# Splitting the first two output tiles of the second MLP product, adding weight pairs by DMA, and moving statistics and small tiles in a one-core decoder block

## Chip, cores and metric

The kernel runs on one core of one Trainium2 chip. The metric is the device time of one execution in microseconds (us). The kernel before was run three times: 751.61, 751.81 and 756.94 us, median 751.81 us.

## What is computed

One decoder block on 512 tokens of width 1024, in float32. A causal pooling mixer and a causal differential attention are merged by sigmoid gates, a cross-attention on a memory of 256 rows follows, then the MLP and a final norm. What bears on the change is the end:

```python
    x = x + memory_cross_attention(hc, mem_n, w_cq[l], w_ckv[l], w_co[l])
    hm = rms_norm(x, g_mlp[l])
    x = x + jnp.square(jax.nn.relu(hm @ w_up[l])) @ w_down[l]
return rms_norm(x, g_final)
```

w_up is 1024 x 4096 and w_down 4096 x 1024.

## The kernel before

Activations stand transposed: 128 features on the partitions, 512 tokens along a row. Every float32 operand is split into a high part (float32r, a cast on ScalarE, `S.copy` in `split`, line 110) and a low part (the difference, on VectorE, line 111), and every product takes three matmuls: high by high, high by low, low by high (`mm3`, lines 104 to 106).

**The MLP** is done in NG = 4 groups of 1024 hidden features. The first product of a group is two sets, n = 2g and 2g+1. A set is a Winograd form of the 2 x 2 block product: seven block products instead of eight. Its left factors are blocks of the weights and sums of them, in the order `ORDER` (for n = 0 `FIRST_ORDER`): A11, s1 = A21 + A22, s2 = s1 + A11, s3 = A21 + A11, A12, A22, s4 = s2 + A12. The names fit the code and not the signs, which lie in the right factors. The four sums are made by VectorE in `combined` (lines 169, 170, 174, 178) from raw blocks that SyncE's DMA queue loads into the tiles `mraw` (five buffers); s1 and s2 stand in `wraw` (three buffers), which also takes the raw weights of all other products. `prep` then splits each block into a pair of tiles, `whi`/`wlo` (three buffers each) or `mhl` (four, so two pairs). `weights(i)` is called when block i comes up on TensorE: it asks for loads up to seven blocks ahead and for splits up to four blocks ahead; five split blocks fit, so a split waits until the block five places before it has been used.

The right factors (B11, T1, T2, T3, B21, B22, T4) are made by `right_factors(m, t)` for each of the eight feature tiles m as the cross-attention's output product (`projection("co", ...)`) finishes it: for m < 4, B11 and T1; for m >= 4, T2 and T3 (lines 772 and 773 and a split), B21 and B22 (a split), T4 (line 781 and a split). `accumulate` adds the tile's squares to `ss2`. After the last tile `split_sq` splits ss2, and `stats2` sums it over the partitions by two matmuls with a matrix of ones (lines 230, 231) and makes 1/rms, `r2`. TensorE's order is the order of the code. `stats2` is put into it by a count of steps, `after(STAT2, ...)`: a block product is four steps, so with STAT2 = 8 it comes after the first two block products (A11 and s1). The order on the other engines is laid out by the compiler's planner, and each of them runs its queue strictly in that order.

`up_set` adds up the seven products (line 871), multiplies by r2 and takes the square of the positive part (`squared_relu`, lines 846 and 847), and splits the result into `act`: entries 0 to 3 from the even set, 4 to 7 from the odd one. Entries 6 and 7 are complete after A22, entries 4 and 5 only after s4, the set's last block.

The second product of a group ("dn") has eight output tiles m. Each is 24 matmuls of 512 columns over act 0 to 7 in order, into one of two PSUM banks `acc`; then `residual` (line 567) adds it to the running x. In the last group tile 7 is done in two halves, with the final norm behind it.

Of the kernel before, what the change touches and what calls it, by code (L numbers as in the profile page):

```python
# [14 lines left out]
ALU = mybir.AluOpType  # L15
# [17 lines left out]
MEMIN, EARLY, LATE = 16, [4, 5, 6, 0, 1], [2, 7, 3]  # L33
WARM = 8
ON_POOL = (1, 3, 5, 7), (1, 3, 5)
STAT1, STAT2, STATM = 16, 8, 20
PARTS = "A11", "A12", "A21", "A22"
ORDER = "A11", "s2", "s1", "s3", "A12", "A22", "s4"
FIRST_ORDER = "A11", "s1", "s2", "A12", "s3", "A22", "s4"
# [10 lines left out]
def block_kernel(ctx: ExitStack, tc: tile.TileContext, x0g, xT, memT, wv, wm, wst, wckv, wpool, vecs, csts, outT):  # L50
# [24 lines left out]
    def sb(tag, shape, bufs, dt=F32):  # L75
        p = apool if tag in EARLY_TAGS else late["pool"] if tag in LATE_TAGS else pool
        return p.tile(shape, dt, tag=tag, name=nm(tag), bufs=bufs)
# [13 lines left out]
    def acc():  # L91
        return ps("acc", 2)
# [16 lines left out]
    def split(hi, lo, src, eng=V):  # L109
        S.copy(hi, src)  # L110
        eng.tensor_tensor(lo, src, f(hi), op=ALU.subtract)  # L111

    vx = sb("vx", [P, NG_COL + T + 19], 1)[:, :NG_COL + T]
    vec = vx[:, :NG_COL]
    cst = sb("cst", [P, NCST], 1)
    nc.sync.dma_start(vx, x0g)
# [6 lines left out]
    warm = ps("acc", 2)  # L123
    for j in range(WARM):
        nc.tensor.matmul(warm, idle[:, :P], idle, start=j == 0, stop=j == WARM - 1)
    eps = sb("eps", [P, 32], 1)[:, :1]
    V.memset(eps, EPS)
    one_f = sb("onef", [P, P], 1)
    V.memset(one_f, 1.0)
# [14 lines left out]
    def fetch(key, src, tag, bufs):  # L144
        if key not in raw:
            raw[key] = sb(tag, [P, D], bufs)
            nc.sync.dma_start(raw[key], src)
        return raw[key]

    def load(i):  # L150
        if i >= len(blocks):
            return
        if isinstance(blocks[i], tuple):
            n, name = blocks[i]
            for part in {"A11": ("A11",), "s1": ("A21", "A22"), "s2": ("A21", "A22"), "A12": ("A12",)}.get(name, ()):
                fetch((n, part), wst[4 * n + PARTS.index(part)], "mraw", 5)
        elif i == 0 and i not in raw:
            r = raw[i] = sb("wraw", [P, D], 3)
            nc.sync.dma_start(r[:, :T], blocks[i][:, :T])
            load_x(1)  # L160
            nc.sync.dma_start(r[:, T:], blocks[i][:, T:])
        else:
            fetch(i, blocks[i], "wraw", 3)

    def combined(n, name):

        if (n, "s1") not in raw and name in ("s1", "s2"):
            s1, s2 = sb("wraw", [P, D], 3), sb("wraw", [P, D], 3)
            V.tensor_tensor(s1, raw[n, "A21"], raw[n, "A22"], op=ALU.add)
            V.tensor_tensor(s2, s1, raw[n, "A11"], op=ALU.add)  # L170
            raw[n, "s1"], raw[n, "s2"] = s1, s2
        elif name == "s3":
            r = raw[n, "A21"]
            V.tensor_tensor(r, r, raw[n, "A11"], op=ALU.add)
            return r
        elif name == "s4":
            r = raw[n, "s2"]
            V.tensor_tensor(r, r, raw[n, "A12"], op=ALU.add)
            return r
        return raw[n, name]  # L180
# [52 lines left out]
    def rstd_full(sp, scratch, w=T):  # L233
        o = ps("tr", 2)[:, :w]
        bcast_sum(o, *sp)
        r = sb("rstd" if w == T else "mrstd", [P, w], 1)
        rsqrt(r, o, 1.0 / D, scratch, tmp()[:, :w])
        return r

# [11 lines left out]
    def accumulate(ss, k, src, w=T):  # L251
        if k == 0:
            S.activation(ss, src, AF.Square)
        else:
            sq = tmp()[:, :w]
            S.activation(sq, src, AF.Square)
            V.tensor_tensor(ss, ss, sq, op=ALU.add)
# [28 lines left out]
    def tile_mm(o, w, rhs, ks=range(KC), first=True, last=True):  # L286
        ks = list(ks)
        for n, k in enumerate(ks):
            c = slice(k * P, (k + 1) * P)
            mm3(o, w[0][:, c], w[1][:, c], rhs[k][0], rhs[k][1],  # L290
                first and n == 0, last and n == len(ks) - 1)
            tick()
# [60 lines left out]
    def lambdas():  # L353
        lvec = tmp()[:, :NVEC]
        nc.gpsimd.dma_start(lvec, vecs)
        lam = sb("lam", [P, 4], 1)
        lsum = sb("lsum", [P, 4], 1)
        for j in range(2):
            b = 128 * j
            V.tensor_tensor(lvec[:, b:b + 64], lvec[:, b:b + 64], lvec[:, b + 64:b + 128], op=ALU.mult)  # L360
            V.tensor_reduce(lsum[:, j:j + 1], lvec[:, b:b + 64], axis=AX.X, op=ALU.add)
            S.activation(lam[:, j:j + 1], lsum[:, j:j + 1], AF.Exp)
        V.tensor_tensor(lam[:, 2:3], lam[:, 0:1], lam[:, 1:2], op=ALU.subtract)
        V.tensor_scalar(lam[:, 3:4], lam[:, 2:3], LAM_INIT, None, op0=ALU.add)
        gsub = sb("gsub", [P, 16], 1)[:, :1]
        V.tensor_scalar(gsub, vec[:, GSUB:GSUB + 1], 1.0 - LAM_INIT, None, op0=ALU.mult)
        st["lam"], st["gsub"] = lam[:, 3:4], gsub

# [196 lines left out]
    def residual(m, o, g=None, ss=None, nxt=None, tag=None):  # L565
        t = res[m]
        V.tensor_tensor(t, o, t, op=ALU.add)  # L567
        if ss is None:
            return
        pr = pair(tag, 8)  # L570
        scaled(pr[:, 0, :], pr[:, 1, :], t, vec[:, g + m:g + m + 1])
        accumulate(ss, m, t)
        nxt[m] = (pr[:, 0, :], pr[:, 1, :])
# [168 lines left out]

    ss2 = sb("ss", [P, T], 1)
    right = {n: {} for n in ("B11", "T1", "B21", "B22", "T2", "T3", "T4")}
    xs, half = {}, {}
    A, B = slice(0, M), slice(M, T)

    def parts(name, k, hi, lo, c):
        right[name][k] = (hi[:, c], lo[:, c])

    def right_factors(m, t):

        k = m % 4
        g = vec[:, G_MLP + m:G_MLP + m + 1]
        x = tmp()
        pr = pair("mix", 8)
        if m < 4:
            if k % 2 == 0:
                half["B12"] = tmp()
            b12 = half["B12"][:, k % 2 * M:k % 2 * M + M]  # L760
            S.activation(x[:, A], t[:, A], AF.Copy, scale=g)
            S.activation(b12, t[:, B], AF.Copy, scale=g)
            V.tensor_tensor(x[:, B], x[:, A], b12, op=ALU.subtract)
            xs[k] = (x[:, B], b12)
            split(pr[:, 0, :], pr[:, 1, :], x)
            parts("B11", k, pr[:, 0, :], pr[:, 1, :], A)
            parts("T1", k, pr[:, 0, :], pr[:, 1, :], B)
            return
        S.activation(x, t, AF.Copy, scale=g)
        t1, b12 = xs[k]  # L770
        y = tmp()
        V.scalar_tensor_tensor(y[:, A], x[:, B], -1.0, t1, op0=ALU.mult, op1=ALU.subtract)
        V.tensor_tensor(y[:, B], x[:, B], b12, op=ALU.subtract)
        p2 = pair("s", 6)
        split(p2[:, 0, :], p2[:, 1, :], y)
        parts("T2", k, p2[:, 0, :], p2[:, 1, :], A)
        parts("T3", k, p2[:, 0, :], p2[:, 1, :], B)
        split(pr[:, 0, :], pr[:, 1, :], x)
        parts("B21", k, pr[:, 0, :], pr[:, 1, :], A)
        parts("B22", k, pr[:, 0, :], pr[:, 1, :], B)  # L780
        V.scalar_tensor_tensor(y[:, A], y[:, A], -1.0, x[:, A], op0=ALU.mult, op1=ALU.subtract)
        if k % 2 == 0:
            half["T4"] = pair("s", 6)
        c = slice(k % 2 * M, k % 2 * M + M)
        split(half["T4"][:, 0, c], half["T4"][:, 1, c], y[:, A])
        parts("T4", k, half["T4"][:, 0, :], half["T4"][:, 1, :], c)

    def done_co(m, o):
        residual(m, o)
        right_factors(m, res[m])  # L790
        accumulate(ss2, m, res[m])

    def renew():

# [65 lines left out]
    def up_set(n, act, j0):  # L860
# [12 lines left out]
        for name in FIRST_ORDER if n == 0 else ORDER:  # L873
# [23 lines left out]
            elif name == "s4":  # L897
                u["C12"] = u["U4"]
                plus("C12", o, "U4")
                squared_relu(*x, u["C12"], B)  # L900

    for g in range(NG):
        act = {}
        for n in (2 * g, 2 * g + 1):
            up_set(n, act, 4 * (n % 2))
        for m in range(KC):
            last = g == NG - 1
            w = W("dn", g, m)
            if last and m % 2 == 0:
                y3[m // 2] = sb("mix", [P, 2, T], 8)  # L910
            if last and m == KC - 1:
                st["sp3"] = split_sq(ss3, T)
                for hf, o in enumerate((ps("sc", 3), ps("sc", 3))):
                    c = slice(hf * M, (hf + 1) * M)
                    tile_mm(o[:, c], w, {k: (a[:, c], b[:, c]) for k, (a, b) in act.items()})
                    last_rows(m, o, c)
                flush()
                continue
            o = acc()
            tile_mm(o, w, act)  # L920
            residual(m, o)
            if last:
                accumulate(ss3, m, res[m])
                S.activation(y3[m // 2][:, m % 2, :], res[m], AF.Copy,
                             scale=vec[:, G_FINAL + m:G_FINAL + m + 1])


def _mtiles(w):
# [70 lines left out]
```

## Time and profile before

| | |
|---|---|
| median of 3 runs | 751.81 us |
| profiled execution, its time | 758.01 us |
| profiled execution, its span | 756.2 us |
| mean granted TensorE clock | 0.978 |
| TensorE busy | 722.5 us (96%) |
| VectorE busy | 530.7 us (70%) |
| ScalarE busy | 393.9 us (52%) |
| GpSimd busy | 58.8 us (8%) |
| moved by DMA | 78.51 MB |

In the profile PE is TensorE's matmul, PEld its weight load, DVE VectorE, ACT ScalarE, POOL GpSimd and SP SyncE; SPq and POOLq are the issuing queues. L111 is line 111 of the kernel. A wait's row gives who waited (engine, tile, line), for whom, the total, the number of times and the longest. A window's row gives each engine's busy time in that stretch with the number of its instructions, the granted clock and the DMA engines' share. Matmuls overlap in their pipeline, so a matmul's duration (0.39 us) is longer than the distance between two of them (0.23 us).

### The profile page before, as it was taken

The numbers are of one execution on the slowest core, as the hardware profiler recorded it, in microseconds if no ns is written. First come the engines' busy times: TensorE is split into PE (matmuls) and PEld (weight loads), VectorE is DVE, ScalarE is ACT, GpSimd is POOL, SyncE is SP. The second block draws the span as 40 slices with busy tenths as digits, with TensorE's granted clock in tenths as the row PEclk, the third lists the DMA queues.
The fourth block names the chain that finished last, engine by engine and source line by source line (L and its number), as shares of the span: only waits on it lengthen the run. The fifth ranks groups of instructions, "written<-read, shape, count | busy, mean of one in ns | idle before, by whom it ended". The sixth has DMA issues, their size and how long they took to land.

```text
span 756.2 us, 10215 instructions
## 1 busy us (share of the span) xinstructions
PE 722.5 (96%) x3960; PEld 623.4 (82%) x3960; DVE 530.7 (70%) x813; ACT 393.9 (52%) x641; POOL 58.8 (8%) x50
## 2 busy tenths in 40 slices
PE   8999999999999999999969899998999989998993
PEld 6878788788889888888869888997889968898883
DVE  7586999875987556556999844797448963688326
ACT  7497998676765434445656512364125621265322
POOL 0053112543000000000000000000000000000003
PEclk9999999999999999999989999999999999999997
DMA  8443223251535531205123500453004610115003
GB/s 308 137 120 103 82 73 111 72 174 63 195 102 177 193 115 56 84 29 195 56 84 115 193 1 28 140 167 112 29 29 140 195 56 28 56 56 168 1 1 111
DMA packets 24657, 78.51 MB, mean 104 GB/s; under 512 B 2689, under 2 KB 4737, under 8 KB 24609
## 3 DMA queue, kind: packets, MB, share of 16 engines
q1 hardware_dynamic: 24560, 77.73, 31.6%
q8 instruction: 31, 0.51, 0.3%
q14 instruction: 18, 0.14, 0.1%
q0 software_dynamic: 48, 0.13, 0.0%
HBM read 73.65 MB, written 2.10 MB: 100 GB/s over the span
## 4 chain that ended last, share of the span: by engine, by line
PE 75%; DVE 16%; ACT 5%; issue 2%; DMA 1%; POOL 0%; SPq 0%; DVEq 0%
PE acc L105 15%; PE acc L104 15%; PE acc L106 15%; PE sc L104 8%; PE sc L105 8%; PE sc L106 8%; DVE wlo L111 3%; DVE tmp L871 2%; DVE xg L111 1%; DVE mhl L111 1%; DVE tmp L846 1%; DVE mix L111 1%; ACT tmp L442 1%; DMA tmp<-xT 1%; DVE mix L835 1%
## 5 line engine op out<-in xcount | busy, mean ns | idle before, releaser
L110 ACT CAST whi<-wraw 128x1024 fp32r<-128x1024 f32 (+1 forms) x98 | 102.3, 1045 | 134.9 <-PE acc L105 63.8
L104 PE MATMUL acc<-xg,whi 128*128 128x512 f32 x400 | 160.3, 401 | 4.1 <-ACT xg L110 4.1
L105 PE MATMUL acc<-xg,whi 128*128 128x512 f32 x400 | 158.3, 396 | 0.5 <-DVE xg L111 0.5
L106 PE MATMUL acc<-xg,wlo 128*128 128x512 f32 x400 | 158.0, 395 | 0.0
L111 DVE TENSOR_TENSOR wlo<-wraw,whi 128x1024 fp32r<-128x1024 f32 (+1 forms) x98 | 121.3, 1238 | 27.5 <-ACT whi L110 26.8
L104 PEld LDWEIGHTS acc<-xg,whi 128*128 128x128 f32 x400 | 76.3, 191 | 20.3 <-ACT xg L110 4.9
L106 PEld LDWEIGHTS acc<-xg,wlo 128*128 128x128 f32 x400 | 76.3, 191 | 16.5
L105 PEld LDWEIGHTS acc<-xg,whi 128*128 128x128 f32 x400 | 76.4, 191 | 15.9 <-DVE xg L111 1.1
L567 DVE TENSOR_TENSOR vr<-acc,vr 128x512 f32<-128x512 f32 x41 | 28.3, 691 | 86.1 <-PE acc L106 86.1
L106 PE MATMUL sc<-mix,wlo 128*128 128x256 f32 (+1 forms) x192 | 56.8, 296 | 0.0
L104 PE MATMUL sc<-mix,whi 128*128 128x256 f32 (+1 forms) x192 | 56.8, 296 | 0.0
L105 PE MATMUL sc<-mix,whi 128*128 128x256 f32 (+1 forms) x192 | 56.7, 295 | 0.0
L835 POOL TENSOR_TENSOR mix<-mix,tmp 128x256 f32<-128x256 f32 x7 | 6.1, 905 | 560.8 <-ACT mix L817 559.5
L110 ACT CAST mhl<-wraw 128x1024 fp32r<-128x1024 f32 x22 | 23.1, 1050 | 48.2 <-PE acc L105 32.4
L104 PE MATMUL acc<-xg,mhl 128*128 128x512 f32 x104 | 42.6, 409 | 4.0 <-ACT xg L110 4.0
L105 PE MATMUL acc<-xg,mhl 128*128 128x512 f32 x104 | 42.5, 409 | 0.3 <-DVE xg L111 0.2
L871 DVE TENSOR_TENSOR tmp<-sc,tmp 128x512 f32<-128x512 f32 x56 | 37.8, 686 | 6.4 <-PE sc L106 5.7
L106 PE MATMUL acc<-xg,mhl 128*128 128x512 f32 x104 | 42.0, 404 | 0.0
L110 ACT CAST whi<-mraw 128x1024 fp32r<-128x1024 f32 x19 | 20.0, 1050 | 38.7 <-PE acc L105 23.3
L104 PEld LDWEIGHTS sc<-mix,whi 128*128 128x128 f32 x192 | 36.2, 188 | 1.2
L105 PEld LDWEIGHTS sc<-mix,whi 128*128 128x128 f32 x192 | 36.1, 188 | 1.2
L106 PEld LDWEIGHTS sc<-mix,wlo 128*128 128x128 f32 x192 | 36.1, 188 | 1.1
(270 smaller groups left out, 1703.0 us busy)
## 6 DMA issues: line engine op xcount, KB each, us to landing
wraw<-wm SPq DMA_DIRECT2D x76, 512.0 KB, 3.3
mraw<-wst SPq DMA_DIRECT2D x32, 512.0 KB, 3.5
wraw<-wckv SPq DMA_DIRECT2D x16, 512.0 KB, 3.4
s<-s SPq DMA_DIRECT2D x8, 256.0 KB, 3.8
vr<-xT SPq DMA_DIRECT2D x8, 256.0 KB, 4.9
outT<-mix SPq DMA_DIRECT2D x8, 256.0 KB, 2.2
tmp<-xT SPq DMA_DIRECT2D x7, 256.0 KB, 7.2
wraw<-wv SPq DMA_DIRECT2D x3, 512.0 KB, 7.0
```

What stands on the lines that cost most here:

```text
L104: nc.tensor.matmul(o, lh, rh, start=start, stop=False)
L105: nc.tensor.matmul(o, lh, rl, start=False, stop=False)
L106: nc.tensor.matmul(o, ll, rh, start=False, stop=stop)
L110: S.copy(hi, src)
L111: eng.tensor_tensor(lo, src, f(hi), op=ALU.subtract)
L442: S.activation(e[:, :n], e[:, :n], AF.Exp, bias=mn, scale=-1.0, accum_out=sm[:, c:c + 1])
L567: V.tensor_tensor(t, o, t, op=ALU.add)
L835: eng.tensor_tensor(y3[j][:, i, c], y3[j][:, i, c], r, op=ALU.mult)
L846: V.scalar_tensor_tensor(t, t, 0.0, r, op0=least, op1=ALU.mult)
L871: V.tensor_tensor(u[new], o, u[old], op=ALU.add)
```

## The change

- Of the four sums of a set, s1 and s3 are no longer made by VectorE. SyncE's queue loads A22 (for s1, into `wraw`) and A21 (for s3, into `mraw`), and GpSimd's queue issues a DMA that adds A21, or A11, from device memory onto it. s2 and s4 stay on VectorE. A set now loads seven blocks of 512 KB instead of four.
- In `right_factors`, for m >= 4, T2 and T3 come first; the split of x (B21, B22) and T4 are a function `right_rest`, which runs at once for tiles 4 and 5, and for 6 and 7 only after the squares of tile 7 have been added.
- STAT2 goes from 8 to 13: the sums over ss2 come one step into the fourth block product (A12).
- In the second product, tiles 0 and 1 each do act 0 to 3 first, into the two `acc` banks; then tile 0 and tile 1 do act 6, 7, 4, 5. The other tiles are as before.
- Small tiles get other homes: eps stands in a column of the tile of x and the gains, the lambda sums and the scaled gain share one tile, and the memory's 1/rms has a wider one.

```diff
-STAT1, STAT2, STATM = 16, 8, 20
+STAT1, STAT2, STATM = 16, 13, 20
...
-            for part in {"A11": ("A11",), "s1": ("A21", "A22"), "s2": ("A21", "A22"), "A12": ("A12",)}.get(name, ()):
-                fetch((n, part), wst[4 * n + PARTS.index(part)], "mraw", 5)
+            if (n, "A11") not in raw:
+                fetch((n, "A11"), part(n, "A11"), "mraw", 5)
+            if (n, "s1") not in raw and name in ("s1", "s2"):
+                r = fetch((n, "s1"), part(n, "A22"), "wraw", 3)
+                nc.gpsimd.dma_start(r, part(n, "A21"), accum_op=ALU.add)
+            if (n, "s3") not in raw and name == "s3":
+                r = fetch((n, "s3"), part(n, "A21"), "mraw", 5)
+                nc.gpsimd.dma_start(r, part(n, "A11"), accum_op=ALU.add)
+            if name in ("A12", "A22"):
+                fetch((n, name), part(n, name), "mraw", 5)
...
-        if (n, "s1") not in raw and name in ("s1", "s2"):
-            s1, s2 = sb("wraw", [P, D], 3), sb("wraw", [P, D], 3)
-            V.tensor_tensor(s1, raw[n, "A21"], raw[n, "A22"], op=ALU.add)
-            V.tensor_tensor(s2, s1, raw[n, "A11"], op=ALU.add)
-            raw[n, "s1"], raw[n, "s2"] = s1, s2
-        elif name == "s3":
-            r = raw[n, "A21"]
-            V.tensor_tensor(r, r, raw[n, "A11"], op=ALU.add)
-            return r
+        if name == "s2":
+            r = raw[n, "s2"] = sb("wraw", [P, D], 3)
+            V.tensor_tensor(r, raw[n, "s1"], raw[n, "A11"], op=ALU.add)
...
-        split(pr[:, 0, :], pr[:, 1, :], x)
         parts("B21", k, pr[:, 0, :], pr[:, 1, :], A)
         parts("B22", k, pr[:, 0, :], pr[:, 1, :], B)
+        if m < KC - 2:
+            right_rest(k, x, y, pr)
+        else:
+            rest.append((k, x, y, pr))
+
+    def right_rest(k, x, y, pr):
+        split(pr[:, 0, :], pr[:, 1, :], x)
         V.scalar_tensor_tensor(y[:, A], y[:, A], -1.0, x[:, A], op0=ALU.mult, op1=ALU.subtract)
...
         accumulate(ss2, m, res[m])
+        if m == KC - 1:
+            for r in rest:
+                right_rest(*r)
...
+            if m < 2:
+                o = acc()
+                tile_mm(o, w, act, range(4), True, False)
+                begun.append((o, w))
+                if m == 0:
+                    continue
+                for i, (o, w) in enumerate(begun):
+                    tile_mm(o, w, act, (6, 7, 4, 5), False, True)
+                    finish(i, o, last)
+                continue
             o = acc()
             tile_mm(o, w, act)
-            residual(m, o)
-            if last:
-                accumulate(ss3, m, res[m])
-                S.activation(y3[m // 2][:, m % 2, :], res[m], AF.Copy,
-                             scale=vec[:, G_FINAL + m:G_FINAL + m + 1])
+            finish(m, o, last)
```

More of the change, by code (lines that the diff above doesn't have):

```diff
@@ L111, in split @@
         eng.tensor_tensor(lo, src, f(hi), op=ALU.subtract)
-    vx = sb("vx", [P, NG_COL + T + 19], 1)[:, :NG_COL + T]
+    home = sb("vx", [P, 608], 1)
+    vx = home[:, :NG_COL + T]
     vec = vx[:, :NG_COL]
@@ L125, in block_kernel @@
         nc.tensor.matmul(warm, idle[:, :P], idle, start=j == 0, stop=j == WARM - 1)
-    eps = sb("eps", [P, 32], 1)[:, :1]
+    eps = home[:, 560:561]
     V.memset(eps, EPS)
@@ L148, in fetch, with part @@
         return raw[key]
+    def part(n, name):
+        return wst[4 * n + PARTS.index(name)]
     def load(i):
@@ L235, in rstd_full @@
         bcast_sum(o, *sp)
-        r = sb("rstd" if w == T else "mrstd", [P, w], 1)
+        r = sb("rstd", [P, w], 1) if w == T else sb("mrstd", [P, w + 48], 1)[:, :w]
         rsqrt(r, o, 1.0 / D, scratch, tmp()[:, :w])
@@ L355, in lambdas @@
         nc.gpsimd.dma_start(lvec, vecs)
-        lam = sb("lam", [P, 4], 1)
-        lsum = sb("lsum", [P, 4], 1)
+        few = sb("lam", [P, 16], 1)
+        lam, lsum, gsub = few[:, :4], few[:, 4:8], few[:, 8:9]
         for j in range(2):
@@ L364, in lambdas @@
         V.tensor_scalar(lam[:, 3:4], lam[:, 2:3], LAM_INIT, None, op0=ALU.add)
-        gsub = sb("gsub", [P, 16], 1)[:, :1]
         V.tensor_scalar(gsub, vec[:, GSUB:GSUB + 1], 1.0 - LAM_INIT, None, op0=ALU.mult)
@@ L744, in block_kernel @@
     right = {n: {} for n in ("B11", "T1", "B21", "B22", "T2", "T3", "T4")}
-    xs, half = {}, {}
+    xs, half, rest = {}, {}, []
     A, B = slice(0, M), slice(M, T)
@@ L900, in up_set, with finish @@
                 squared_relu(*x, u["C12"], B)
+    def finish(m, o, last):
+        residual(m, o)
+        if last:
+            accumulate(ss3, m, res[m])
+            S.activation(y3[m // 2][:, m % 2, :], res[m], AF.Copy, scale=vec[:, G_FINAL + m:G_FINAL + m + 1])
     for g in range(NG):
-        act = {}
+        act, begun = {}, []
         for n in (2 * g, 2 * g + 1):
```

## The prediction

> **What bounds the kernel now.** First the page's table of engines, then TensorE's own waits in the second half (from 340 us).
>
> ```profile
> PE 722.5 (96%) x3960; PEld 623.4 (82%) x3960; DVE 530.7 (70%) x813; ACT 393.9 (52%) x641; POOL 58.8 (8%) x50
> ```
> ```profile
> PE acc L104 <- ACT xg L110: 8.1, 4, 2.1
> PE tr L230 <- ACT tmp L110: 5.1, 1, 5.1
> PE tr L231 <- DVE tmp L111: 1.0, 1, 1.0
> ...
> PE acc L105 <- DVE xg L111: 0.7, 3, 0.2
> ```
>
> TensorE is the bound; what can be won without fewer matmuls is its waits and what they bring. There are five: at the start of each group's second product (L104 and L105 for act) and at the statistics (L230 and L231 for ss2's halves). Next I asked for windows around them, and for undisturbed windows beside them.
>
> ```profile
> 430.00:438.00 8.00, 5.90 (x18) 4.11 (x17) 3.27 (x5) 1.89 (x4) 0.00 (x0) 0.79 0.35 122
> 518.50:526.50 8.00, 5.76 (x18) 4.08 (x17) 2.98 (x4) 1.74 (x4) 0.00 (x0) 0.79 0.30 107
> 607.00:615.00 8.00, 5.71 (x17) 4.03 (x16) 2.80 (x4) 1.70 (x4) 0.00 (x0) 0.79 0.26 92
> 695.50:703.50 8.00, 5.77 (x17) 4.02 (x17) 2.86 (x4) 1.70 (x4) 0.00 (x0) 0.79 0.30 99
> ...
> 384.00:397.00 13.00, 6.96 (x37) 6.15 (x36) 11.42 (x21) 7.05 (x13) 0.00 (x0) 0.74 0.36 122
> 398.00:411.00 13.00, 13.00 (x112) 13.00 (x111) 11.98 (x16) 6.66 (x9) 0.00 (x0) 1.00 0.26 82
> ```
> ```profile
> 444.00:460.00 16.00, 16.00 (x72) 13.23 (x72) 6.79 (x7) 2.83 (x4) 0.00 (x0) 1.00 0.11 34
> ```
>
> The first numbers in brackets are matmuls. Undisturbed, the second product issues 72 in 16 us, 4.5 per us. In the four windows 18, 18, 17 and 17 were issued in 8 us: 4.0, 4.0, 3.8 and 3.8 us of work, so 4.0 + 4.0 + 4.2 + 4.2 = **16.4 us lost**. That is more than the waits: the granted clock is 0.79 there. Around the statistics 37 matmuls, two of double width (so 39), went out where 112 go undisturbed: 39/112 x 13 = 4.5 us of work, **8.5 us lost**, at a clock of 0.74. Together 24.9 us; the rest of TensorE's time the change doesn't touch.
>
> The clock shows in the chain at the first start: 0.43 us between matmuls after the wait, 0.23 some 3 us later.
>
> ```profile
> 428.96 0.68 DVE xg L111
> 429.64 0.60 DVE tmp L871
> 430.24 1.13 DVE wlo L111
> 431.38 0.61 DVE tmp L846
> ...
> 432.01 0.64 ACT tmp L847
> ...
> 432.67 0.63 ACT xg L110
> ...
> 433.32 0.70 DVE xg L111
> ...
> 435.29 0.43 PE acc L104
> ...
> 437.97 0.23 PE acc L106
> ```
>
> [...]
>
> **The starts of the second product.** The chain above is the end of a set: the C21 half split at 428.96 (entries 6, 7), then L871, a weight split, L846, the square, two splits, done at 434.02. The matmuls begin here:
>
> ```profile
> 428.36 0.39 PE L104 MATMUL acc<-xg,mhl 128*128 128x512 f32 x1
> ```
>
> Before, entry 4 is asked for after four k, 12 matmuls, 12/4.5 = 2.7 us: at 431.0, 3.0 us too early. In the new order act 0 to 3 of two tiles come first, 24 matmuls or 5.3 us, so entries 6 and 7 are asked for at 433.7 (ready at 429.6) and entry 4 after six more, 6.7 us from the start, at 435.1. Even if VectorE is as late as now, it is ready 1.0 us before; no new wait follows. The matmuls are the same in number. What else moves: both acc banks are held until tile 0 has finished, and tile 2 begins 16 k after the start, one tile's second half after tile 0 is done and long after its residual of 0.7 us. The weights of tile 0 are held 2.7 us longer, and the split five blocks on with them. I take the whole 16.4 us.
>
> **The weight sums.** Up to the statistics VectorE is full:
>
> ```profile
> 349.00:392.00 43.00, 36.96 (x185) 31.02 (x183) 42.33 (x62) 30.33 (x48) 0.00 (x0) 0.97 0.23 74
> ```
> ```profile
> L174 DVE TENSOR_TENSOR mraw<-mraw,mraw 128x1024 f32<-128x1024 f32 x2 | 2.5, 1227 | 0.0
> L169 DVE TENSOR_TENSOR wraw<-mraw,mraw 128x1024 f32<-128x1024 f32 x2 | 2.5, 1226 | 0.0
> ```
>
> 42.33 of 43 us. The four sums of the first two sets go, 4 x 1.13 us from one to the next = 4.5 us. Sixteen go in all, but the other twelve lie where VectorE has slack, so I count nothing for them beyond making the chain at the starts surer. What they cost instead is 16 adding DMAs and three more loads per set (24 x 512 KB = 12.6 MB, on 78.5 MB).
>
> No adding DMA is in this trace. The nearest rows:
>
> ```profile
> L355 POOL DMA_DIRECT2D tmp<-vecs x1: 701/701/701, 15.4 to 15.4; - x1
> ```
> ```profile
> mraw<-wst SPq DMA_DIRECT2D x32, 512.0 KB, 3.5
> ...
> tmp<-vecs POOLq DMA_DIRECT2D x1, 128.0 KB, 3.8
> ```
>
> Bounds: a plain load's 3.5 us from below, and from above 3.8 us for a quarter of the bytes times four, 15.2 us. I take 7 us, twice the plain load, since it reads two operands. On TensorE's path it costs nothing as long as it lands in time, because GpSimd's queue holds nothing else after the attention. The tightest place is the first set of a group:
>
> ```profile
> 439.09 1.23 DVE L111 TENSOR_TENSOR mhl<-wraw,mhl 128x1024 fp32r<-128x1024 f32 x1 [0.16 <-ACT mhl L110]
> ...
> 459.90 1.05 ACT L110 CAST whi<-wraw 128x1024 fp32r<-128x1024 f32 x1 [4.39 <-PE acc L105]
> ```
>
> The first row ends the use of the buffer that s1 takes over, at 440.3, and 2.7 us later in the new order; a load of 3.5 us follows, until 446.5. The second row casts s2 = s1 + A11, whose sum takes 1.2 us. So the adding DMA has 459.9 - 1.2 - 446.5 = **12.2 us**. At 7 us it is hidden. At 15.2 it is 3 us late; then the sum for s2 and a residual queued behind it on VectorE wait, which two acc banks of 24/4.5 = 5.3 us each still bear.
>
> [...]
>
> **The statistics.** The rows around them:
>
> ```profile
> 381.96 0.70 DVE L567 TENSOR_TENSOR vr<-acc,vr 128x512 f32<-128x512 f32 x1
> ...
> 388.18 0.70 DVE L111 TENSOR_TENSOR mix<-tmp,mix 128x512 fp32r<-128x512 f32 x1
> ...
> 389.38 0.43 DVE L781 SCALAR_TENSOR_TENSOR tmp<-tmp,tmp 128x256 f32<-128x256 f32 x1
> ...
> 391.79 1.37 DVE L111 TENSOR_TENSOR s<-tmp,s 128x256 fp32r<-128x256 f32 x3
> ```
> ```profile
> 379.00 0.40 PE L106 MATMUL acc<-xg,wlo 128*128 128x512 f32 x1
> ...
> 384.83 0.28 PE L106 MATMUL sc<-mix,wlo 128*128 128x256 f32 x1
> ```
>
> TensorE ends the projection at 379.2 and A11 and s1 at 384.9. The last tile's residual comes at 381.96, its T2 split, the first of the three at 391.79, ends about 392.4. s2 wants this T2 after nine matmuls (13/112 us each), at 386.0; A12 follows at 387.7, with the moved statistics six matmuls in, at 388.4. The 4.5 us taken off VectorE bring the residual to 379.4 at the earliest, 2.6 us sooner, and leave 1.9 us less queue behind it; deferred work takes another 0.6 (the split at 388.18) and twice 0.34 (L781) from in front: 392.4 - 5.8 = 386.6 for T2, 0.6 late. What is late next is the deferred split of x of tiles 6 and 7, which A12 needs from 388.4 on: two splits of 0.6 us on VectorE, each behind a cast, with the squares' sum (0.6) and the split of ss2 (0.6) competing: 388.5 to 390. So I leave 2.5 us of the 8.5 (1.5 of wait, 1 of slow clock) and count **6.0 us**. If VectorE keeps its order as before, nothing is gained; at best all 8.5.
>
> The lambda and eps homes change no operation; eps may now wait for the x load, which the first product waits for anyway: zero.
>
> **Sum.** 16.4 + 6.0 = 22.4 us: 758.0 to 735.6 for the profiled execution. That execution is 6.2 us above the median of 751.8; the waits are a planner's order and not its slowness, so I take them off the median: **729.4 us**, 3.0% faster.
>
> **Rivals.**
> - *The statistics' wait only moves* to A12 and its x splits, and the clock falls again. For it: VectorE's full window. Against it: 4.5 us less work. Gain 16.4 alone: 735.4. Chance 0.17.
> - *The starts are only half won*: the planner puts other work (such as the 1.13 us weight split above) before the last L846, so entry 4 misses its 1.0 us of slack. Half of 16.4 plus 6.0: 737.6. Chance 0.11.
> - *Nothing at the end*: sums land some 15 us after their load, ScalarE and VectorE, in strict order, stand before the first sets' sums in the full window and at the starts, and what is won is given back. 744 to 759. Chance 0.09.
> - *Slower, by late sums.* Beyond 12.2 + 5.3 = 17.5 us per adding DMA each further us holds the residuals and so TensorE, at four groups. To eat 22.4 us it needs 5.6 us more per group, 23 us; to be 1% slower (7.5 us), 25 us. At 27 us: 751.8 - 22.4 + 4 x 9.5 = 767. That lies beyond my upper bound of 15.2. Chance 0.08.
>
> The forecast, all waits gone but a remainder at the statistics, has 0.55: 725 to 734. The range is 723 (more than all 24.9 us, by the noise of a few us) to 745, which takes in the first two rivals. A measurement of this kernel tells about 1%, 7.5 us, from no change: faster by more 0.83, within 0.09, slower 0.08.
>
> **What would show it.** The four waits L104 <- ACT xg are gone and windows after each start keep a clock of 1.00; L230 waits under 1 us, or not, with a wait at L104 on mix or s in its place; the sums L169 and L174 are missing from VectorE, with 16 GpSimd DMAs landing in under 12 us. I am wrong if those DMAs take over 17 us, if VectorE shows waits on a DMA in the stage before the statistics, or if VectorE still ends a set over 6.7 us after the second product began.

## The result and the profile after

| | before | after |
|---|---|---|
| median of 6 runs each | 754.78 us | **736.81 us** |
| lowest to highest | 751.61 to 756.94 | 736.63 to 738.22 |
| profiled execution, its time | 758.01 us | 736.63 us |
| its span | 756.2 us | 734.5 us |
| mean granted TensorE clock | 0.978 | 0.986 |
| moved by DMA | 78.51 MB | 91.09 MB |

The ratio is 0.9774, 95% interval 0.9749 to 0.9799: 2.3% faster, where 3.0% was forecast. The time lies in the range, 7.4 us above the forecast.

First the page's table of engines, then TensorE's waits from 340 us on.

```profile
PE 706.9 (96%) x3960; PEld 613.9 (84%) x3960; DVE 512.8 (70%) x797; ACT 392.6 (53%) x641; POOL 72.7 (10%) x66
```
```profile
PE sc L105 <- DVE s L111: 4.6, 2, 2.8
PE sc L104 <- ACT s L110: 3.3, 2, 3.1
PE acc L104 <- DVE vr L572: 1.0, 1, 1.0
```

The waits at the starts of the second product (L104 on xg) are gone, and so are those of the statistics (L230, L231 of before). In their place TensorE waits four times for `s`, the right factors T2 that s2 needs (the first set runs in the order A11, s1, s2, A12, s3, A22, s4, so s2 is its third product), and once for a residual (vr) to free an accumulator. Windows of 8 us behind the four starts, and two around the statistics:

```profile
428.50:436.50 8.00, 8.00 (x36) 6.38 (x35) 5.64 (x9) 4.08 (x6) 0.00 (x0) 1.00 0.39 131
511.80:519.80 8.00, 8.00 (x37) 6.63 (x36) 4.42 (x7) 2.96 (x5) 0.00 (x0) 1.00 0.34 121
594.90:602.90 8.00, 8.00 (x37) 6.61 (x36) 4.42 (x7) 2.99 (x5) 0.00 (x0) 1.00 0.32 115
678.10:686.10 8.00, 8.00 (x37) 6.64 (x36) 4.42 (x7) 3.37 (x7) 0.00 (x0) 1.00 0.35 125
382.50:397.50 15.00, 7.12 (x34) 6.08 (x33) 13.07 (x23) 9.20 (x15) 0.00 (x0) 0.66 0.32 106
398.00:411.00 13.00, 13.00 (x117) 13.00 (x117) 11.46 (x16) 6.37 (x8) 0.86 (x1) 1.00 0.52 127
```

At the starts 36 or 37 matmuls stand where 17 or 18 stood, at a clock of 1.00. Around the statistics the clock is 0.66 over 15 us, where it was 0.74 over 13: that place has become worse.

To see where the time went I read from the timeline when TensorE begins each stage: the last five tiles of the output product (projection), the first group's first product with the statistics in it, the four second products, the other three first products, and the rest. In us:

| kernel | ahead | projection | first product with statistics | second products | first products 2 to 4 | rest |
|---|---|---|---|---|---|---|
| before | 352.0 | 27.2 | 49.1 | 187.8 | 120.1 | 19.9 |
| after | 348.4 | 28.4 | 50.0 | 169.0 | 118.7 | 19.9 |
| begin_only | 349.3 | 27.2 | 48.7 | 170.6 | 120.1 | 19.9 |
| adds_only | 349.4 | 27.9 | 54.5 | 188.1 | 120.1 | 19.9 |
| homes_only | 348.7 | 27.2 | 48.6 | 185.1 | 118.7 | 19.9 |
| sums_on_vector | 348.7 | 27.2 | 48.5 | 168.8 | 118.7 | 19.9 |
| early_statistics | 348.8 | 27.2 | 48.9 | 168.8 | 118.7 | 19.9 |
| no_deferral | 348.8 | 27.2 | 49.0 | 168.8 | 118.7 | 19.9 |
| weights_after_factors | 349.9 | 27.2 | 43.9 | 169.4 | 118.7 | 19.9 |
| early_adds | 348.4 | 27.2 | 47.1 | 168.8 | 118.7 | 19.9 |
| both | 348.9 | 27.2 | 45.3 | 168.8 | 118.7 | 19.9 |
| shifted | 348.9 | 27.2 | 47.2 | 170.8 | 115.3 | 19.9 |
| both_and_home | 349.0 | 27.2 | 44.2 | 170.9 | 115.3 | 19.9 |

(The names are those of the experiments below.) From the projection on, after is 18.1 us shorter than before: 18.8 less in the second products, 1.4 less in the first products, 2.1 more in projection and statistics. The 3.6 us ahead of them belong to the profiled execution of before, and mostly to a stretch with a slower clock (other executions with the same code there have 349.3 and 349.4 us, not 352.0; weights_after_factors, with 349.9, also has a clock of 0.96 from 40 to 80 us); the two medians differ by 18.0 us. The window of before:

```profile
40.00:80.00 40.00, 37.87 (x167) 30.97 (x167) 31.55 (x54) 33.55 (x65) 15.38 (x12) 0.96 0.34 104
```

Why the statistics lost: VectorE's largest wait between 340 and 400 us, then the instructions around it in the timeline, and TensorE's first matmul of the first product.

```profile
DVE wraw L181 <- DMA wraw<-wst: 8.2, 2, 5.3
```
```profile
353.44 0.33 SPq L148 DMA_DIRECT2D wraw<-wst  x1
...
358.87 0.86 POOL L163 DMA_DIRECT2D wraw<-wst  x1 [0.40 <-DVE mix L111]
...
365.72 1.23 DVE L181 TENSOR_TENSOR wraw<-wraw,mraw 128x1024 f32<-128x1024 f32 x1 [5.35 <-DMA wraw<-wst]
...
378.29 1.23 DVE L181 TENSOR_TENSOR wraw<-wraw,mraw 128x1024 f32<-128x1024 f32 x1 [2.86 <-DMA wraw<-wst]
...
385.45 0.68 DVE L572 TENSOR_TENSOR vr<-acc,vr 128x512 f32<-128x512 f32 x1
...
392.27 1.02 DVE L111 TENSOR_TENSOR s<-tmp,s 128x512 fp32r<-128x512 f32 x2
```
```profile
376.85 0.28 PE L104 MATMUL sc<-mix,mhl 128*128 128x256 f32 x1
```

L181 is s2 = s1 + A11. VectorE comes to it at 360.4 (365.72 less 5.35), and s1's load was issued only at 353.44, when its `wraw` buffer came free; the adding DMA was issued at 358.87, some 2 us after a load of 3.3 us would have landed (its row names an instruction of VectorE as the last that it waited for), and its sum was there at 365.72. What came behind it in VectorE's queue stood too, ready or not: a split of `mix` whose cast on ScalarE was done at 360.85 began only at 368.00. So the right factors stood behind it for 5.35 us, and again for 2.86 us at the second set: 8.2 us, where the four sums taken off had cost 4.5 us. So the last tile's residual came at 385.45, 8.6 us after TensorE was done with the projection, where before it was 2.7 (381.96 after 379.2). The last T2, in the row at 392.27, was there at 393.0.

The DMA view (KB each, median us to landing):

```profile
mraw<-wst SPq DMA_DIRECT2D x32, 512.0 KB, 3.4
...
mraw<-wst POOLq DMA_DIRECT2D x8, 512.0 KB, 5.7
wraw<-wst SPq DMA_DIRECT2D x8, 512.0 KB, 3.3
wraw<-wst POOLq DMA_DIRECT2D x8, 512.0 KB, 5.8
```

An adding DMA takes 5.7 or 5.8 us where a plain load takes 3.3 or 3.4: inside the prediction's bounds and under its 7. (No run has a plain load of this size from GpSimd's queue, so what the queue and what the adding costs isn't told apart.)

### The profile page after: what moved, and what is told of

Read it like the earlier page. It is cut to its first block, busy times and chain, and to the rows that moved or that the text cites. A ratio compares the mean times of both kernels' runs of the same rounds, so it can differ in the third digit from the quotient of the medians.

```text
span 734.5 us, 10275 instructions
## 1 busy us (share of the span) xinstructions
PE 706.9 (96%) x3960; PEld 613.9 (84%) x3960; DVE 512.8 (70%) x797; ACT 392.6 (53%) x641; POOL 72.7 (10%) x66
## 2 busy tenths in 40 slices
DMA packets 28112, 91.09 MB, mean 124 GB/s; under 512 B 3072, under 2 KB 5120, under 8 KB 28064
## 4 chain that ended last, share of the span: by engine, by line
PE 80%; DVE 7%; DMA 5%; ACT 4%; issue 2%; POOL 0%; SPq 0%; DVEq 0%; POOLq 0%
PE acc L104 16%; PE acc L106 15%; PE acc L105 15%; PE sc L104 9%; PE sc L106 9%; PE sc L105 9%; DMA wraw<-wst 2%; DMA mraw<-wst 2%; DVE wlo L111 1%; ACT tmp L447 1%; DVE mix L849 1%; DMA tmp<-xT 1%; DVE tmp L445 1%; PE sc L386 1%; ACT tmp L417 1%
## 5 line engine op out<-in xcount | busy, mean ns | idle before, releaser
L104 PE MATMUL acc<-xg,whi 128*128 128x512 f32 x400 | 158.2, 396 | 1.0 <-DVE vr L572 1.0
L106 PE MATMUL acc<-xg,wlo 128*128 128x512 f32 x400 | 156.1, 390 | 0.0
L105 PE MATMUL acc<-xg,whi 128*128 128x512 f32 x400 | 155.8, 390 | 0.0
L104 PEld LDWEIGHTS acc<-xg,whi 128*128 128x128 f32 x400 | 75.2, 188 | 16.0 <-ACT whi L110 1.3
L105 PEld LDWEIGHTS acc<-xg,whi 128*128 128x128 f32 x400 | 75.2, 188 | 14.6
L104 PE MATMUL sc<-mix,whi 128*128 128x256 f32 (+1 forms) x192 | 56.5, 294 | 0.0
L105 PE MATMUL acc<-xg,mhl 128*128 128x512 f32 x104 | 40.6, 390 | 0.0
L104 PE MATMUL acc<-xg,mhl 128*128 128x512 f32 x104 | 40.5, 389 | 0.0
L106 PE MATMUL acc<-xg,mhl 128*128 128x512 f32 x104 | 40.5, 389 | 0.0
L110 ACT CAST whi<-mraw 128x1024 fp32r<-128x1024 f32 x19 | 20.0, 1051 | 38.3 <-PE acc L105 21.8
L104 PEld LDWEIGHTS sc<-mix,whi 128*128 128x128 f32 x192 | 36.3, 189 | 1.0
L105 PE MATMUL sc<-s,whi 128*128 128x256 f32 x104 | 30.1, 290 | 4.6 <-DVE s L111 4.6
```

The costliest lines, as they stand in the source:

```text
L104: nc.tensor.matmul(o, lh, rh, start=start, stop=False)
L105: nc.tensor.matmul(o, lh, rl, start=False, stop=False)
L106: nc.tensor.matmul(o, ll, rh, start=False, stop=stop)
```

## The experiments

Each was timed in five rounds beside the kernel before, whose median was 755.96 us beside begin_only, adds_only, sums_on_vector and first_sums_on_vector, 755.77 beside weights_after_factors, early_adds, no_deferral and shifted, and 755.91 beside early_statistics, homes_only, both and both_and_home. Ratios are to that.

### begin_only: the new order of tiles 0 and 1 by itself

```diff
 # before, and in the loop over the output tiles of the second product:
+            if m < 2:
+                o = acc()
+                tile_mm(o, w, act, range(4), True, False)
+                begun.append((o, w))
...
+                    tile_mm(o, w, act, (6, 7, 4, 5), False, True)
```

> The kernel before with only the new order of tiles 0 and 1 in the second product; sums on VectorE, statistics and factors as before. Theory (the new order alone hides the end of a set): the four waits of L104 on xg are gone, clock 1.00 after each start, 17 to 19 us under before; the wait at L230 stays at 5 us. Rival (the waits go only because VectorE has less to add): half of them stay, 8 to 10 us under before.

737.80 us, ratio 0.9767 (0.9743 to 0.9791): 18.2 us by the medians, 17.2 in the second products by the table. TensorE's waits from 340 us:

```profile
PE tr L230 <- ACT tmp L110: 5.1, 1, 5.1
PE tr L231 <- DVE tmp L111: 1.0, 1, 1.0
PE tr L823 <- ACT tmp L816: 0.7, 1, 0.7
```

The starts' waits are gone and the statistics' are untouched. This one part alone is worth all that the whole change is worth; the others add up to nothing.

### adds_only: the adding DMAs by themselves

```diff
 # before, with load() and combined() of the changed kernel
+                r = fetch((n, "s1"), part(n, "A22"), "wraw", 3)
+                nc.gpsimd.dma_start(r, part(n, "A21"), accum_op=ALU.add)
```

> The kernel before with only the adding DMAs for s1 and s3. Theory (VectorE stands before the adds of the first two sets): waits of VectorE on the adds of 5 to 9 us before the statistics, TensorE's wait at L230 longer by 2 to 5 us, the four waits at the starts as before or a little shorter: 0 to 5 us over before. Rival (the four sums taken off VectorE help): the wait at L230 shorter by 3 to 5 us, 3 to 6 us under before.

761.19 us, ratio 1.0078 (1.0056 to 1.0099), 5.2 us **slower**, where 0 to 5 were expected. TensorE's first wait from 340 us, then VectorE's:

```profile
PE tr L235 <- ACT tmp L110: 9.4, 1, 9.4
```
```profile
DVE wraw L180 <- DMA wraw<-wst: 19.6, 5, 4.8
```

Of VectorE's 19.6 us two waits, 7.9 us, stand ahead of the statistics. TensorE's wait for them grew from 5.1 to 9.4 us, and the stage from 49.1 to 54.5.

### sums_on_vector and first_sums_on_vector: the sums back on VectorE

```diff
 # the changed kernel, with load() and combined() of before: all sums on VectorE
```
```diff
 # the changed kernel, but for the first two sets
+        if n < 2:
+            # s1 and s3 loaded and summed as in the kernel before
```

> The changed kernel, but all sums s1 and s3 made by VectorE as before; the order of tiles, statistics, deferral and homes as changed. Theory (the adding DMAs for s1 of the first two sets let VectorE stand 5.3 + 2.9 = 8.2 us in the stage before the statistics, against 4.5 us of work saved): T2 comes some 4 us earlier, TensorE's waits on s (7.9 us) fall to 4 us or less, 4 to 6 us under the changed kernel, 22 to 24 under before. Rival (the deferral and the planner's order keep T2 late whatever makes the sums): within 1.5 us of the changed kernel.

> The changed kernel, but the sums of the first two sets made by VectorE as before, those of the later six by adding DMAs. Theory (only the adds of the first two sets cost): within 1 us of the kernel with all sums on VectorE. Rival (VectorE's 8 us of waits for adds in the later sets cost too): slower than that kernel by 1.5 us or more. If the deferral is at fault, within 1.5 us of the changed kernel.

733.38 us (ratio 0.9710, 0.9686 to 0.9733) and 733.48 us (0.9709, 0.9685 to 0.9733): both 3.4 us under the changed kernel, where 4 to 6 were expected; the waits on `s` fell from 7.9 to 5.2 us and not to 4. Only the adding DMAs of the first two sets cost time. In the second kernel VectorE still waits 8.8 us for the later sets' DMAs, and that costs nothing. VectorE in sums_on_vector, from the last tile's residual to its T2:

```profile
378.62 0.69 DVE L570 TENSOR_TENSOR vr<-acc,vr 128x512 f32<-128x512 f32 x1
379.22 1.22 DVE L111 TENSOR_TENSOR wlo<-mraw,whi 128x1024 fp32r<-128x1024 f32 x1
...
381.30 1.22 DVE L182 TENSOR_TENSOR wraw<-wraw,mraw 128x1024 f32<-128x1024 f32 x1
382.43 1.22 DVE L111 TENSOR_TENSOR mhl<-mraw,mhl 128x1024 fp32r<-128x1024 f32 x1
...
386.38 1.22 DVE L111 TENSOR_TENSOR wlo<-wraw,whi 128x1024 fp32r<-128x1024 f32 x1
...
387.85 0.68 DVE L111 TENSOR_TENSOR s<-tmp,s 128x512 fp32r<-128x512 f32 x1
```

The residual comes 6.8 us sooner than in the changed kernel, and T2 4.4 us sooner, at 388.5. Still it is late, since four passes over weights (wlo, mhl and the sum at L182), 4 x 1.13 = 4.5 us, stand between the two.

### weights_after_factors: these passes behind the last T2

```diff
 # sums_on_vector, and
+        with tc.issue_after(getattr(st["t2"], "ins", st["t2"])) if 3 <= i - FIRST_UP < 7 else ExitStack():
+            prepare(i)
+
+    def prepare(i):      # the sum and the split of a block: here A12, s3, A22 and s4 of the first set
...
-        split(p2[:, 0, :], p2[:, 1, :], y)
+        st["t2"] = split(p2[:, 0, :], p2[:, 1, :], y)
```

> The kernel with all sums on VectorE, and besides VectorE's splits and sums of the weight blocks A12, s3, A22 and s4 of the first set are queued behind the last T2 split (an order of issue alone). Theory (T2 is late because the planner fills VectorE's gaps with weight work, four instructions of 1.13 us = 4.5 us ahead of the last T2, and the queue is strict): TensorE's waits on s fall from 5.2 us to 1.5 or less, no slow clock at the statistics, 4 to 7 us under the kernel with all sums on VectorE (726 to 729). Rival (the wait only moves on, to the weights that now come later): within 1.5 us of it.

729.55 us, ratio 0.9663 (0.9640 to 0.9686), 3.8 us under sums_on_vector, where 4 to 7 were expected. The residual and the last T2, and then TensorE's one wait between 340 and 410 us:

```profile
377.33 0.69 DVE L574 TENSOR_TENSOR vr<-acc,vr 128x512 f32<-128x512 f32 x1 [0.21 <-PE acc L106]
...
380.70 0.69 DVE L111 TENSOR_TENSOR s<-tmp,s 128x512 fp32r<-128x512 f32 x1
```
```profile
PE sc L104 <- DVE tmp L887: 2.3, 1, 2.3
```

The last T2's split begins 3.4 us after the residual in place of 9.2, and no matmul waits for `s` any more. What is late next is an addition of the products (L887), which now stands behind weight passes: 2.3 us, and the granted clock is still 0.83 from 388 to 398 us, where none below 1.00 was expected. The stage falls from 48.5 to 43.9 us, and 0.6 of it comes back in the first second product.

### early_adds: the same adding DMAs with a buffer that is free early

```diff
 # the changed kernel, and
-                r = fetch((n, "s1"), part(n, "A22"), "wraw", 3)
+                r = fetch((n, "s1"), part(n, "A22"), *(("mraw", 5) if n < 2 else ("wraw", 3)))
```

> The changed kernel, but s1 of the first two sets is loaded and added in the tiles mraw, whose buffers are free from the start of the stage, instead of wraw. Theory (an adding DMA costs only what VectorE stands before it, and it lands late because its buffer comes free late): VectorE's waits on adds before the statistics fall from 8.2 to 3 us or less and the time to that of the kernel with all sums on VectorE or up to 4 us under it (729 to 734). Rival (the adding DMAs cost in another way, by their traffic or their queue): within 1.5 us of the changed kernel (737).

730.49 us, ratio 0.9681 (0.9657 to 0.9705): 6.3 us under the changed kernel, with all 16 adding DMAs in place, and 2.9 under the version with the sums on VectorE. VectorE's wait for them between 340 and 400 us is 2.8 us, once:

```profile
DVE wraw L181 <- DMA mraw<-wst: 2.8, 1, 2.8
```

From 355 to 402 us VectorE now makes one s2 from the adding DMAs (L181), at 365.45, where the changed kernel makes two, at 365.72 and 378.29: the first set's, which had stood for 5.35 us, is done ahead of that. So it isn't the DMA's 5.8 us that hurt but when its buffer came free.

### no_deferral and early_statistics: the two parts of "later statistics"

```diff
 # sums_on_vector, and
-        if m < KC - 2:
+        if m < KC:
```
```diff
 # sums_on_vector, and
-STAT1, STAT2, STATM = 16, 13, 20
+STAT1, STAT2, STATM = 16, 8, 20
```

> The kernel with all sums on VectorE, with the x split and T4 of tiles 6 and 7 not deferred. Theory (the deferral moves only three short instructions of VectorE, while the weight work stays ahead): T2 1 to 1.5 us later, 0.5 to 2.5 us over the kernel with all sums on VectorE. Rival (the deferral is what keeps the stage from being longer): 4 us over it or more.

> The changed kernel with all its sums on VectorE and the statistics at 8 steps again. Theory (the later statistics only trade one wait for another): TensorE's wait of some 5 us for the statistics is back, the waits of 4.4 and 0.8 us for the second factors are gone or under 1 us, and the time is 732.5 to 735 us, beside 733.4 with the statistics late. Rival (the later statistics are worth the 6 us that the prediction gave them, once the sums are back on VectorE): about 739 us.

734.12 us (0.9720, 0.9696 to 0.9743) and 734.33 us (0.9717, 0.9696 to 0.9739): 0.7 and 1.0 us over sums_on_vector, about what these rounds can tell from nothing. With the early statistics TensorE's waits from 340 us are those of before:

```profile
PE tr L234 <- ACT tmp L110: 5.1, 1, 5.1
PE tr L235 <- DVE tmp L111: 1.6, 1, 1.6
```

In sums_on_vector they are these instead:

```profile
PE sc L105 <- DVE s L111: 4.4, 2, 2.6
PE sc L104 <- ACT s L110: 0.8, 1, 0.8
```

6.7 us of waiting for the statistics against 5.2 for the factors, and stages of 48.9 and 48.5: the wait was moved, not removed. homes_only below, which has neither part and the same homes, has a stage of 48.6.

### homes_only, shifted: the homes of the tiles

```diff
 # before, and only the homes of the change:
-    eps = sb("eps", [P, 32], 1)[:, :1]
+    eps = home[:, 560:561]
...
-        r = sb("rstd" if w == T else "mrstd", [P, w], 1)
+        r = sb("rstd", [P, w], 1) if w == T else sb("mrstd", [P, w + 48], 1)[:, :w]
```
```diff
 # sums_on_vector, and mraw and mhl 128 bytes lower:
-        r = sb("rstd", [P, w], 1) if w == T else sb("mrstd", [P, w + 48], 1)[:, :w]
+        r = sb("rstd", [P, w], 1) if w == T else sb("mrstd", [P, w + 16], 1)[:, :w]
```

> The kernel before with only the homes of the tiles changed, as the changed kernel has them (the tiles s and mix start 64 bytes lower, mhl 128 bytes higher); order, sums and statistics as before. Theory (the pace of the matmuls follows the homes): first-product stages of 39.6 us in place of 40.0 and second-product stages 0.3 to 0.6 us shorter each, 2.5 to 4 us in all, so 752 to 753.5 us where the kernel before takes about 756. Rival (the pace came with the new order or with the sums, and the homes do nothing): stages as before, within 1 us of the kernel before.

> The kernel with all sums on VectorE, and the tile of the memory's 1/rms 128 bytes smaller, so that the tiles mraw and mhl, placed behind it, start 128 bytes lower, as in the kernel before (mhl at 211584 instead of 211712 bytes, the one not a multiple of 256). Nothing else differs. Theory (TensorE is slower on operands that start off a multiple of 256 bytes): 256-column matmuls at 0.119 us instead of 0.1178 in the first products, the later first products 40.0 us each instead of 39.6, second products 0.3 to 0.6 us longer, 2 to 4 us over that kernel in all. Rival (the faster pace has to do with the order of work): the same paces and times.

homes_only took 749.81 us, ratio 0.9924 (0.9907 to 0.9941): **6.1 us** less with not one instruction changed, more than the 2.5 to 4 expected. shifted took 730.50 us (0.9677, 0.9653 to 0.9700): 2.9 us under sums_on_vector, where the theory, matmuls slower on operands that start off a multiple of 256 bytes, expected 2 to 4 us more. The first matmul of the second group's first product and of the second product that follows it, in before, homes_only and shifted (there with one in between):

```profile
476.54 0.28 PE L104 MATMUL sc<-mix,whi 128*128 128x256 f32 x1
...
516.62 0.39 PE L104 MATMUL acc<-xg,whi 128*128 128x512 f32 x1
```
```profile
472.41 0.28 PE L104 MATMUL sc<-mix,whi 128*128 128x256 f32 x1
...
511.99 0.40 PE L104 MATMUL acc<-xg,whi 128*128 128x512 f32 x1
```
```profile
467.50 0.28 PE L104 MATMUL sc<-mix,whi 128*128 128x256 f32 x1
...
473.15 0.28 PE L104 MATMUL sc<-mix,mhl 128*128 128x256 f32 x1
...
505.79 0.39 PE L104 MATMUL acc<-xg,whi 128*128 128x512 f32 x1
```

From the first row to the last the same 336 matmuls take 40.1, 39.6 and 38.3 us. In the compiled kernels `mhl` starts 128, 0 and 128 bytes past a multiple of 256, `s` and `mix` 128, 64 and 64, and `whi`, `wlo` and `xg` 0 in all three.

In the second product the pace goes by the operand. Here are the starts of three output tiles of the second group, in before and in homes_only; the first has its weights in `whi` and `wlo`, the other two in `mhl`:

```profile
531.95 0.39 PE L104 MATMUL acc<-xg,whi 128*128 128x512 f32 x1
...
537.39 0.40 PE L104 MATMUL acc<-xg,mhl 128*128 128x512 f32 x1
...
542.98 0.39 PE L104 MATMUL acc<-xg,mhl 128*128 128x512 f32 x1
```
```profile
527.45 0.39 PE L104 MATMUL acc<-xg,whi 128*128 128x512 f32 x1
...
532.89 0.39 PE L104 MATMUL acc<-xg,mhl 128*128 128x512 f32 x1
...
538.33 0.39 PE L104 MATMUL acc<-xg,mhl 128*128 128x512 f32 x1
```

A tile of 24 matmuls takes 5.44 us from `whi` and `wlo` in both (0.2267 us each, start to start); from `mhl` it takes 5.59 us before (0.233) and 5.44 in homes_only. In shifted, with `mhl` at 128 bytes again, it is 5.58, as in both_and_home. So for this product the theory holds, and it gave the 0.3 to 0.6 us a stage that were expected.

In the first product it falls. A matmul of 256 columns takes 0.1192 us before and 0.1178 in homes_only. In shifted the first 48 matmuls of the stage take 0.1178 too, and all those from 473.15 on 0.1133, also the ones that read `whi`, though only `mraw` and `mhl` had moved. The other two first products turn in the same way, after five and after three block products of 24 matmuls. The homes are the only edit, and both_and_home below shows the same gain again, so they do change this pace; but two paces occur with the same homes, and no run tells what turns the one into the other.

In homes_only 4.6 of the 6.1 us are in the stages of the table: 1.4 and 0.5 in the first products and 2.7 in the second ones. 1.6 of the 2.7 are one start, the third, told of at the end. Of the rest 0.6 lies ahead of the stages (348.7 for 349.3 and 349.4 with the old homes); 0.9 I can't place.

### both, both_and_home: the best parts together

```diff
 # early_adds and weights_after_factors together; both_and_home also has [P, w + 16]
```

> The changed kernel with two edits at once: the first two sets' s1 loaded and summed in a buffer that is free early, so that the sum lands before VectorE wants it, and the weight work of the later products of the first set issued behind the last second factor. Theory (what VectorE does ahead of the second factors sets the time, so what is taken from it adds up until TensorE's waits are gone): the 2.3 us that TensorE still waited with the second edit alone shrink, 727 to 729 us. Rival (the second edit alone has already taken all that there was): 729.5 us, with TensorE's wait of 2.3 us still there.

> The kernel with both edits, and mraw and mhl 128 bytes lower. Theory (homes set the pace, stage by stage): first-product stages of about 38.4 us in place of 39.6, second-product stages 0.3 to 0.6 us longer, so 2 to 3.5 us less than the same kernel without this shift. Rival (the 3 us of the earlier shift were chance of that build): within 1 us of it.

730.23 us (0.9664, 0.9643 to 0.9685) and **727.88 us** (0.9635, 0.9615 to 0.9655), the fastest here, 1.2% under the changed kernel. The first is a miss: nothing below either edit alone. TensorE's waits from 340 us in `both`:

```profile
PE tr L241 <- DVE tmp L111: 3.0, 1, 3.0
PE tr L841 <- ACT tmp L834: 0.7, 1, 0.7
PE sc L105 <- DVE s L111: 0.2, 1, 0.2
```

The 2.3 us that the rival expected to stay are gone, and a wait of 3.0 us for the split of ss2 is there: with 13 steps the statistics are late again, now that the factors are in time. The second is 2.4 us under the first, as the homes' theory said (2 to 3.5), with first products of 38.3 to 38.6 us.

## Why the prediction was right, and where it was wrong

**The starts: right.** The step from 2.7 to 6.7 us of cover held: all four waits are gone and the clock behind them is 1.00. 16.4 us were counted; begin_only shows 17.2 in these stages. The difference lies in the counting: a window also counts the matmuls that only reach into it. The windows of after hold 36, 37, 37 and 37 matmuls for 18, 18, 17 and 17, and the 77 between them are 17.5 us at 0.2267 us each.

**The statistics: wrong,** a loss of 2.1 us where 6.0 of gain were counted. The step that failed is "The tightest place is the first set of a group", and with it the price of nothing on TensorE's path. The slack of 12.2 us was worked out there, at the second group; the first two sets, ahead of the statistics, were not looked at. There the buffer came free at 353.44 and VectorE came to the sum 6.9 us later; a load and an adding DMA take 3.3 + 5.8 us, and with the gap between them it was 12.3. Counted from the end of the projection, the residual was forecast at 0.2 us (379.4 for 379.2) and came at 8.6 (385.45 for 376.85): 8.4 us late, which is the 8.2 us of standing. From there on the forecast was good: 7.2 us from the residual to T2 (379.4 to 386.6), and 7.5 measured (385.45 to 393.0). It is the first rival, with the wait at T2 and not at A12; its 735.4 us lies 1.4 below the median. The sign by which the prediction said it would be wrong, VectorE's waits on a DMA ahead of the statistics, is in the trace.

**Even with the sums in time 6.0 was too much.** With the sums on VectorE, late statistics and deferral together bring 0.1 us of stage (48.5 in sums_on_vector, 48.6 in homes_only). What the step didn't weigh was the 4.5 us of weight passes between residual and T2, which no part of the change moves; weights_after_factors moved them and brought 3.8 us.

**The homes: wrong.** "The lambda and eps homes change no operation ... zero". They change none, and by the stages bring some 3 us: 1.4 in the first products 2 to 4 (120.1 to 118.7) and 1.6 in the second ones (begin_only's 170.6 to 169.0).

**The adding DMA's price: right,** 5.7 to 5.8 us for an estimate of 7. The later sets' waits on it cost nothing, and the slower rival didn't come. The issue itself took GpSimd 0.86 us at 358.87, with VectorE at work beside it (rows of tensor_tensor from 358.74 to 360.37), and 0.86 to 0.88 us at all sixteen, where the one issue of the kernel before took 0.70.

**The sum** was 16.4 + 6.0 + 0 = 22.4. The stages give 17.2 - 2.1 + 3.0 = 18.1. The other 3.0 of the 7.4 us are the base: 751.81 was a median of three, and all later medians of the same kernel are 754.8 to 756.0. The prediction took its gain off the median of 751.6, 751.8 and 756.9 and read the profiled 758.0 as the odd one; most executions lie nearer to that. That the time came out so near the forecast is in part luck: the homes, counted at zero, gave 3.0 us, and without them it would have been about 740.

Open: in the changed kernel the 256-column matmuls behind the statistics run at 0.1133 us in the first group and at 0.1178 in the others, with the same homes; weights_after_factors has the faster pace too, for less than two block products between two waits. No run tells why. In the changed kernel it is worth 1.2 us (257 matmuls, 0.0045 us each), so the waits and the slow clock cost more than the 2.1 us by which the table is longer, and this is a part of why sums_on_vector gained 3.4 us and not 4 to 6.

## What to carry over

A sum made by a DMA has to be started one load and one adding DMA (3.3 and 5.8 us here, 12.3 with the gap between them) ahead of the engine that wants it, so look at every place where it is used, the first ones above all, and ask when its buffer comes free: here the same DMAs cost 3.4 us from one buffer and gained 2.9 from another. When a wait is to be moved, write down what the engine behind it has still to do before each of the next two products; later statistics were worth nothing while the weight passes stood ahead of the factors, and no run has these passes moved with the statistics early. And this kernel, with TensorE busy for 96% of the span, took 6.1 us less with nothing but other homes for its tiles, so try the homes by themselves before crediting an edit that happens to move a tile.

## What the runs showed of the hardware

- **Where a tile of weights started changed the pace of the matmuls of 512 columns that read it.** It was 0.2267 us for weights at a multiple of 256 bytes and about 0.233 at 128 bytes past one; no other offset was tried for them. With 256 columns the same instructions took 0.1133, 0.1178 or 0.1192 us, but there two paces stand one after the other with the same homes, so the address alone doesn't set it. A stage gained or lost 0.6 to 3%.
- **Waits of the same length were not always followed by a slower clock.** homes_only waits 2.14, 2.12, 2.12 and 2.12 us at its four starts. Windows of 10 us from the first and the third:

```profile
427.00:437.00 10.00, 7.73 (x26) 5.65 (x26) 4.82 (x7) 2.30 (x3) 0.00 (x0) 0.83 0.20 68
...
602.00:612.00 10.00, 7.65 (x33) 5.75 (x32) 6.11 (x8) 2.29 (x3) 0.00 (x0) 1.00 0.23 73
```

The granted clock is 0.83 behind the first and 1.00 behind the third, 33 matmuls to 26, and that stage is 1.6 us shorter. In the same windows of the second and fourth start the granted clock was 0.83 too. So waits of 2.1 us came with a slower clock three times out of four, and no run tells what sets the third start apart.
- **A DMA that adds took as long as 1.7 plain loads** (5.7 to 5.8 us from GpSimd's queue against 3.3 to 3.4 from SyncE's for 512 KB), not the two that were taken, and 0.86 to 0.88 us of GpSimd for its issue.
